# Two half blocks of down-projection weights loaded into unused halves of sum tiles, ahead of the plain step that uses them

## The chip, the cores and the metric

The kernel runs on one core of one Trainium2 chip. The metric is the device time in microseconds (us), median of several executions. Before the change it is 1205.56 us (three runs, 1204.94 to 1208.27).

The core has a matrix engine (PE in the profile, with its weight loads as PEld), a vector engine (DVE), a scalar engine (ACT), a general engine (POOL), and SP, which here does nothing but issue loads and stores. Each engine works through its own queue of instructions in order and waits there for what an instruction needs.

## The reference, cut to what matters

The reference is one layer of a hybrid decoder: a combined input projection, retention and mLSTM heads, an output projection, and a gated feed-forward network with a causal convolution. The change lies in the last product of the feed-forward network.

```python
u = rmsnorm(h, norm_ffn)
up = causal_dwconv(u @ w_up, ffn_conv_w, ffn_conv_b)       # 2048 -> 2 x 5632
gate, val = jnp.split(up, [5632], axis=-1)
return h + (jax.nn.silu(gate) * val) @ w_down              # 5632 -> 2048
```

There are 256 output rows, two tiles of 128. A last norm follows, and 16 meta tokens at the front are dropped.

## The kernel before, in words

**Precision.** All products are made from two parts. A block of weights comes from memory as float32 into a tile `wraw`. ACT copies it to a rounded type (`whi`), DVE subtracts that copy from the block and rounds what is left (`wlo`), and PE multiplies three times: high by high, high by low, low by high. So each block of weights costs one load, one copy on ACT, one subtraction on DVE, and its matmuls. `load_w` (L113 to L122) does that for whole blocks; its copy is L119 and its subtraction L121. `split` (L763) does it for other tiles, with the copy at L764 and the subtraction at L766.

**Stages.** The feed-forward network goes in two halves of the hidden width. Each half has an up-projection (weights `wu`) and then a down-projection (weights `wd`). A down-projection goes through two pairs of column blocks, `b = 0` and `b = 2`, each of 512 columns twice. A pair has eleven steps `q`, each over 256 hidden rows.

**Two kinds of steps.** Four of the steps (0, 4, 9, 10) are plain: for each of the two column blocks, `j = 0` and `j = 1`, a block of 128 x 1024 values (512 KB) is loaded by `load_step` (L909, which calls `load_w`) and PE makes 12 matmuls with it, at L828. The other seven (`FAST`: 1, 2, 3, 5, 6, 7, 8) make a Strassen-like step of seven products instead of eight, in `seven` (L830). Such a step loads four parts of weights into one half of the area `left`: one part of 256 KB that was worked out earlier (`kept`, L838), and three parts of 768 KB together (L839). These loads show as `hT` in the profile, since `left` lies where the tile `hT` was. DVE then makes three differences of the parts, two in a tile `ta` of 128 x 1024 (L842) and one in the first half of a tile `tb` of the same size (L843). The second half of `tb` is used by nobody. Four splits (L764 and L766) and 21 matmuls (L857, L858, L860) follow.

So in the order of steps, runs of seven-product steps alternate with plain steps: 0, then 1 2 3, then 4, then 5 6 7 8, then 9 10. The very last pair of the kernel (second half, `b = 2`) has another order, 0 1 4 2 7 3 5 6 8 9 10, with 7 and 8 plain, and the `j = 1` blocks of its last four plain steps are put off to the end.

**What the tiles share.** `wraw`, `ta` and `tb` are all tiles of one ring of four (`name="wraw", bufs=4`). A new one can be written only when the readers of an older one are through. `whi` and `wlo` are rings of five each. `left` has two halves that alternate, so a seven-product step can load only when the step two before it has read its half.

**What sets the order.** The kernel is written in program order, and a planner orders the instructions of each engine by a simulated timeline and adds the waits. `tc.issue_after(x)` adds that an instruction of a block stands behind `x` on the same engine. The planner also orders SP's loads: in the trace, the load of step 5 can stand ahead of the loads of step 4. While a down-projection runs, POOL adds finished results of the pair before to `hn`, by transfers that accumulate (L876).

Of the kernel before, what the change touches and what calls it, by code (L numbers as in the profile page):

```python
# [11 lines left out]
F32R = mybir.dt.float32r  # L12
# [4 lines left out]
P = 128  # L17
# [66 lines left out]
def trunk(ctx: ExitStack, tc: tile.TileContext, io, out: bass.AP):  # L84
    nc = tc.nc

    def pool(name, bufs, **kw):
        return tc.tile_pool(name=name, bufs=bufs, **kw)

    consts = ctx.enter_context(pool("consts", 1, side="left"))  # L90
    wpool = ctx.enter_context(pool("wpool", 1, side="left"))
# [21 lines left out]
    def load_w(src, shape, to=None):  # L113
        nonlocal last_load
        raw = wpool.tile(shape, F32, name="wraw", bufs=4)
        last_load = nc.sync.dma_start(raw, src)
        to, n = (wpool, 5) if to in (None, wpool) else (to, None)
        hi = to.tile(shape, F32R, name="whi", bufs=n)
        nc.scalar.copy(hi, raw)  # L119
        lo = to.tile(shape, F32R, name="wlo", bufs=n)  # L120
        nc.vector.tensor_tensor(out=lo, in0=raw, in1=hi.bitcast(F32), op=ALU.subtract)  # L121
        return hi, lo  # L122
# [83 lines left out]
    with pool("sq", 1, side="right") as sqp:  # L206
        for k0, k1 in [(0, 1), (1, 2)] + [(k, k + 2) for k in range(2, KT, 2)]:
            n = k1 - k0
# [3 lines left out]
            raw = wpool.tile([P, 2, W0], F32, name="wraw", bufs=4)[:, :n, :]  # L212
# [16 lines left out]
            for k in range(k0, k1):  # L229
                i = k - k0  # L230
                first, last = k == 0, k == KT - 1
                for j, (ps, t0) in enumerate(((k_ps, 0), (q_ps, TQ))):
                    w = hi[:, :, j * P : (j + 1) * P], lo[:, :, j * P : (j + 1) * P]
# [36 lines left out]
    with tc.issue_after(parted.ins):  # L270
        a = _COLS["retn"][0]
        nc.vector.tensor_scalar(out=norms[:, :RH], in0=par[:, a : a + RH], scalar1=-0.5, scalar2=None, op0=ALU.mult)

        a = _COLS["mln"][0]
# [318 lines left out]
    NQD = NHF // 2  # L593
# [74 lines left out]
    def x_tile(i):  # L668
        return x5[:, i, :]
# [23 lines left out]
    def squares(tt, i, c0, c1):  # L693

        nc.scalar.activation(junk[:, : c1 - c0], hn[:, tt, c0:c1], AF.Square, scale=DM ** -0.5, accum_out=ss4[:, tt, i : i + 1])

    def times_gain(tt, c0, c1):
        h = hn[:, tt, c0:c1]
        nc.gpsimd.tensor_tensor(out=h, in0=h, in1=gfin[:, c0:c1], op=ALU.mult)
# [44 lines left out]
    for half in range(2):  # L744
# [18 lines left out]
        def split(hi, lo, x, after=None):  # L763
            copied = nc.scalar.copy(hi, x)  # L764
            with tc.issue_after(after.ins) if after else nullcontext():
                return copied, nc.vector.tensor_tensor(out=lo, in0=x, in1=hi.bitcast(F32), op=ALU.subtract)  # L766

        gt = None
        for jj in range(NHF):
            j = half * NHF + jj  # L770
            pair = []
            for s in range(2):
# [7 lines left out]
                if 2 * jj + s in begins:  # L780
                    n = begins.index(2 * jj + s)
                    b, q = units[n]
# [6 lines left out]
            q, i = divmod(jj, 2)  # L789
# [37 lines left out]
            for n, (a, m, i) in list(enumerate(parts))[n0:n1]:  # L827
                nc.tensor.matmul(ps, a, m[:, i, cols], start=first and n == 0, stop=seed or last and n == 5, skip_group_check=seeded)  # L828

        def seven(b, q, cs, ps, first, last, after, norm):  # L830


            nonlocal turn
            f = FAST.index(q)
            raw = left[turn]
            turn = 1 - turn

            nc.sync.dma_start(raw[:, 0, :], early[b, q])  # L838
            nc.sync.dma_start(raw[:, 1:4, :], io["wd7"][b // 2, half * NQD + q][:, 1:4, :])  # L839
            ta, tb = (wpool.tile([P, 2, 512], F32, name="wraw", bufs=4) for _ in range(2))  # L840

            nc.vector.tensor_tensor(out=ta, in0=raw[:, 0:1, :].to_broadcast([P, 2, 512]), in1=raw[:, 1:3, :], op=ALU.subtract)  # L842
            nc.vector.tensor_tensor(out=tb[:, 0, :], in0=raw[:, 3, :], in1=raw[:, 0, :], op=ALU.subtract)  # L843
            copied = None
            for w, to in (
                (raw[:, 2:4, :], ((S4, cs[0, 1], False, False), (A12, cs[0, 0], False, False))),
                (raw[:, 0:2, :], ((S2, ps[2], first, last), (A11, ps[0], first, last))),
                (ta, ((S3, ps[1], first, last), (S1, ps[3], first, last))),
                (tb[:, 0:1, :], ((A22, cs[1, 0], False, False),)),
            ):  # L850
                hi = wpool.tile([P, 2, 512], F32R, name="whi", bufs=5)
                lo = wpool.tile([P, 2, 512], F32R, name="wlo", bufs=5)
                n = len(to)
                with tc.issue_after(after.ins) if first and after else nullcontext():
                    copied, _ = split(hi[:, :n, :], lo[:, :n, :], w)
                for i, (m, o, begin, _) in enumerate(to):
                    nc.tensor.matmul(o, sh[:, f, m, :], hi[:, i, :], start=begin, stop=False)  # L857
                    nc.tensor.matmul(o, sl[:, f, m, :], hi[:, i, :], start=False, stop=False)  # L858
                for i, (m, o, _, end) in enumerate(to):
                    nc.tensor.matmul(o, sh[:, f, m, :], lo[:, i, :], start=False, stop=end)  # L860
            if norm:

                with tc.issue_after(copied.ins):
                    for g in norm:
                        squares(*g)
                reached = nc.gpsimd.tensor_tensor(out=junk[:, 0:1], in0=tb[:, 0, 0:1], in1=tb[:, 0, 0:1], op=ALU.add)
                with tc.issue_after(reached.ins):
                    for tt, _, c0, c1 in norm:
                        times_gain(tt, c0, c1)
# [4 lines left out]
        def onto(tt, b, x):  # L874

            nc.gpsimd.dma_start(block(tt, b), x, accum_op=ALU.add)  # L876

        def share(ps, b, final):

            p1, p7, p6, p5 = ps  # L880
            x6, x7, x5, x1 = (x_tile(i) for i in range(4))
            nc.scalar.copy(x1, p1)  # L882
            onto(0, b, x1)
            nc.vector.tensor_tensor(out=x6, in0=p6, in1=x1, op=ALU.add)
            nc.vector.tensor_tensor(out=x7, in0=p7, in1=x6, op=ALU.add)
            onto(1, b, x7)
            nc.vector.tensor_tensor(out=x6, in0=x6, in1=p5, op=ALU.subtract)
            if final:

                nc.vector.tensor_tensor(out=block(0, b + 1), in0=block(0, b + 1), in1=x6, op=ALU.add)  # L890
            else:
                onto(0, b + 1, x6)
            nc.vector.tensor_tensor(out=x5, in0=x7, in1=p5, op=ALU.subtract)
            onto(1, b + 1, x5)
# [14 lines left out]
        def load_step(b, q, to=wpool):  # L909
            return load_w(io["wd"][b, half * NQD + q], [P, 2, 512], to)  # L910
# [3 lines left out]
        emptied = None  # L914
        for b in (0, 2):
            cs = {}
            for j in range(2):
                for tt in range(2):
                    cs[tt, j] = at.tile([P, 512], F32, name="atps")
            ps = [mm.tile([P, 512], F32, name="mmps") for _ in range(4)]  # L920

            final = half == 1 and b == 2
            steps = [0, 1, 4, 2, 7, 3, 5, 6, 8, 9, 10] if final else range(NQD)
            fast = [q for q in steps if q in FAST and not (final and q in BOTH)]
            plain = [q for q in steps if q not in fast]
            alone = plain[-lag:] if final else []
            for q in steps:
                if q in fast:
                    due = []
                    if final and q != fast[0]:  # L930
                        due, gains = gains[:1], gains[1:]
                    seven(b, q, cs, ps, q == fast[0], q == fast[-1], emptied, due)
                    if q == fast[-1]:
                        with tc.high_priority() if final else nullcontext():
                            share(ps, b, final)
                    continue
                for j in range(2):
                    if j == 1 and q in alone:
                        continue
                    w = load_step(b + j, q)  # L940
                    for tt in range(2):
                        product(cs[tt, j], tt, q, w, q == plain[0], q == plain[-1 - (lag if final and (tt, j) == (1, 1) else 0)])
            for j in range(2):
                for n, tt in enumerate(range(2)):
                    c = (b + j) * 512
                    if not final:

                        x = x_tile((4, 3, 1, 0)[2 * j + n])
                        emptied = nc.scalar.copy(x, cs[tt, j])
                        onto(tt, b + j, x)  # L950
                        if half == 1:
                            gains.append((tt, b + j, c, c + 512))
                    elif j == 0:
                        add(cs[tt, j], tt, c)
                        squares(tt, b, c, c + 512)
                        times_gain(tt, c, c + 512)
# [116 lines left out]
```

## Time and profile before

| | before |
|---|---|
| median of three runs | 1205.56 us |
| profiled execution, its own time | 1206.01 us |
| its span (first to last instruction) | 1204.2 us |
| PE busy | 1194.5 us, 99% of the span |
| DVE busy | 971.1 us, 81% |
| ACT busy | 708.1 us, 59% |
| granted PE clock | 0.998 |
| down-projection, first half, `b = 0` and `b = 2` | about 717.5 to 773 and 773 to 828.5 us |
| down-projection, second half, `b = 0` and `b = 2` | about 1083 to 1138 and 1138 to 1197 us |

The times inside the profile are microseconds from the start of the span. A row such as `wlo<-wraw,whi` names the tile that is written and the tiles that are read. Matmuls overlap each other, so a matmul's own duration is longer than the distance from its start to the next one's start; the distance is what counts for the pace. What stands in square brackets is the idle time before an instruction and what ended it. An "x2" in a row of the timeline means that two instructions of one kind were merged.

### The profile page before, as it was taken

How to read it: one execution, taken by the hardware profiler on the slowest of the kernel's cores; microseconds unless marked ns; L12 is line 12 of the kernel's file. 1: busy time of each engine (PE TensorE's matmuls, PEld its weight loads, DVE VectorE, ACT ScalarE, POOL GpSimd, SP SyncE). 2: the span in 40 equal slices, each digit the busy share in tenths (PEclk: the TensorE clock that was granted, in tenths of full speed). 3: DMA queues.
4: the chain of work that ended last, by engine and by line, in shares of the span. 5: the costliest groups of instructions: out<-in, count | busy, mean ns of one | idle time of the engine just before them, and what ended most of it. 6: DMA issues, size and time to landing. Idle time of an engine off the chain costs nothing.

```text
span 1204.2 us, 22798 instructions
## 1 busy us (share of the span) xinstructions
PE 1194.5 (99%) x8956; PEld 1151.2 (96%) x8956; DVE 971.1 (81%) x1446; ACT 708.1 (59%) x964; POOL 167.3 (14%) x222
## 2 busy tenths in 40 slices
PE   9999999999999999999999999999999999999997
PEld 9999999999999999999999998878999999998886
DVE  8967778766775966788888889997697878789897
ACT  8747746655656656555555556665554655556664
POOL 0100001111110311021112100202023112100232
PEclk9999999999999999999999999999999999999999
DMA  8865565566565965766866744949777767755956
GB/s 280 275 208 162 169 187 169 197 182 192 171 189 168 345 204 176 252 219 203 263 217 212 225 178 175 272 182 272 279 249 250 234 247 242 253 184 211 281 170 200
DMA packets 83005, 263.27 MB, mean 219 GB/s; under 512 B 14673, under 2 KB 18897, under 8 KB 82769
## 3 DMA queue, kind: packets, MB, share of 16 engines
q1 hardware_dynamic: 71952, 223.85, 56.9%
q0 software_dynamic: 10368, 37.11, 10.1%
q8 instruction: 70, 1.15, 0.4%
q10 hardware_dynamic: 576, 0.85, 0.2%
q14 instruction: 39, 0.31, 0.1%
HBM read 243.42 MB, written 11.27 MB: 211 GB/s over the span
## 4 chain that ended last, share of the span: by engine, by line
PE 97%; DMA 1%; DVE 1%; ACT 0%; issue 0%; SPq 0%; DVEq 0%; ACTq 0%
PE mmps L128 26%; PE mmps L129 25%; PE mmps L131 25%; PE atps L828 8%; PE mmps L860 2%; PE mmps L857 2%; PE mmps L858 2%; PE atps L858 1%; PE atps L857 1%; PE atps L860 1%; PE atps L380 1%; DMA wraw<-in_wd 1%; PE atps L372 0%; DMA hT<-in_xT 0%; PE atps L128 0%; PE atps L131 0%
## 5 line engine op out<-in xcount | busy, mean ns | idle before, releaser
L119 ACT CAST whi<-wraw 128x1024 fp32r<-128x1024 f32 x352 | 368.5, 1049 | 311.0 <-PE mmps L129 200.9
L121 DVE TENSOR_TENSOR wlo<-wraw,whi 128x1024 fp32r<-128x1024 f32 x352 | 432.5, 1231 | 68.9 <-ACT whi L119 66.7
L128 PE MATMUL mmps<-uh,whi 128*128 128x258 f32 x1408 | 346.1, 283 | 0.0
L129 PE MATMUL mmps<-ul,whi 128*128 128x258 f32 x1408 | 346.0, 283 | 0.0
L128 PEld LDWEIGHTS mmps<-uh,whi 128*128 128x128 f32 x1408 | 267.6, 190 | 0.1
L129 PEld LDWEIGHTS mmps<-ul,whi 128*128 128x128 f32 x1408 | 267.1, 190 | 0.1
L128 PE MATMUL mmps<-xh,whi 128*128 128x272 f32 (+2 forms) x864 | 219.8, 288 | 0.0
L129 PE MATMUL mmps<-xl,whi 128*128 128x272 f32 (+2 forms) x864 | 218.3, 286 | 0.0
L131 PE MATMUL mmps<-uh,wlo 128*128 128x258 f32 x1408 | 196.5, 282 | 0.0
L131 PEld LDWEIGHTS mmps<-uh,wlo 128*128 128x128 f32 x1408 | 179.9, 189 | 0.0
L129 PEld LDWEIGHTS mmps<-xl,whi 128*128 128x128 f32 x864 | 162.9, 189 | 0.0
L128 PEld LDWEIGHTS mmps<-xh,whi 128*128 128x128 f32 x864 | 162.5, 188 | 0.1
L131 PE MATMUL mmps<-xh,wlo 128*128 128x272 f32 (+2 forms) x864 | 126.6, 285 | 0.0
L131 PEld LDWEIGHTS mmps<-xh,wlo 128*128 128x128 f32 x864 | 114.2, 188 | 0.0
L764 ACT CAST whi<-hT 128x1024 fp32r<-128x1024 f32 x52 | 53.6, 1052 | 26.5 <-PE atps L828 7.9
L681 DVE TENSOR_TENSOR cu<-mmps,rstd 128x258 f32<-128x258 f32 x88 | 37.3, 424 | 38.1 <-PE mmps L131 37.5
L766 DVE TENSOR_TENSOR wlo<-hT,whi 128x1024 fp32r<-128x1024 f32 x52 | 62.2, 1221 | 5.9 <-ACT whi L764 4.7
L129 PE MATMUL mmps<-mixl,whi 128*128 128x258 f32 x256 | 63.0, 283 | 0.0
L128 PE MATMUL mmps<-mixh,whi 128*128 128x258 f32 x256 | 62.4, 282 | 0.0
L766 DVE TENSOR_TENSOR wlo<-wraw,whi 128x1024 fp32r<-128x1024 f32 (+1 forms) x52 | 52.2, 1038 | 0.9 <-PE mmps L860 0.2
L764 ACT CAST whi<-wraw 128x1024 fp32r<-128x1024 f32 (+1 forms) x52 | 43.0, 837 | 16.5 <-PE mmps L858 7.1
L876 POOL DMA_DIRECT2D hn<-x x27 | 23.6, 1033 | 202.6 <-ACT x L882 174.8
(284 smaller groups left out, 1732.9 us busy)
## 6 DMA issues: line engine op xcount, KB each, us to landing
wraw<-in_wu SPq DMA_DIRECT2D x176, 512.0 KB, 4.5
wraw<-in_wi SPq DMA_DIRECT2D x108, 512.0 KB, 4.1
hT<-in_wd SPq DMA_DIRECT2D x26, 768.0 KB, 4.6
wraw<-in_wd SPq DMA_DIRECT2D x36, 512.0 KB, 4.9
wraw<-in_wo SPq DMA_DIRECT2D x32, 512.0 KB, 4.1
x<-in_wd POOLq DMA_DIRECT2D x13, 768.0 KB, 7.5
hn<-x POOLq DMA_DIRECT2D x27, 256.0 KB, 7.9
hT<-kept SPq DMA_DIRECT2D x26, 256.0 KB, 2.8
```

Of the source, the lines that this page charges most:

```text
L119: nc.scalar.copy(hi, raw)
L121: nc.vector.tensor_tensor(out=lo, in0=raw, in1=hi.bitcast(F32), op=ALU.subtract)
L128: nc.tensor.matmul(ps, hi[:, k, :], xh(kk), start=kk == first, stop=False)
L129: nc.tensor.matmul(ps, hi[:, k, :], xl(kk), start=False, stop=False)
L131: nc.tensor.matmul(ps, lo[:, k, :], xh(kk), start=False, stop=kk == last)
L681: evacuated = nc.vector.tensor_tensor(out=u, in0=ps[:, :NQ], in1=rstd2, op=ALU.mult)
L764: copied = nc.scalar.copy(hi, x)
L766: return copied, nc.vector.tensor_tensor(out=lo, in0=x, in1=hi.bitcast(F32), op=ALU.subtract)
L828: nc.tensor.matmul(ps, a, m[:, i, cols], start=first and n == 0, stop=seed or last and n == 5, skip_group_check=seeded)
L857: nc.tensor.matmul(o, sh[:, f, m, :], hi[:, i, :], start=begin, stop=False)
L858: nc.tensor.matmul(o, sl[:, f, m, :], hi[:, i, :], start=False, stop=False)
L860: nc.tensor.matmul(o, sh[:, f, m, :], lo[:, i, :], start=False, stop=end)
```

## The change

The plain step behind a run of at least two seven-product steps no longer loads its `j = 0` block into a `wraw` tile of its own. The block's two halves, 128 x 512 values each (256 KB), go into the unused second halves of the `tb` tiles of the last two steps of that run. Both are asked for in the last step of the run, behind that step's own load on SP. The block is then split in two instructions of 512 columns on ACT and two on DVE in place of one each of 1024. The `j = 1` block is loaded as before.

The condition holds at seven places: step 4 and step 9 in both pairs of the first half and in the first pair of the second half, and step 8 in the last pair. So seven loads of 512 KB become fourteen of 256 KB.

```diff
-        def seven(b, q, cs, ps, first, last, after, norm):
+        def seven(b, q, cs, ps, first, last, after, norm, pieces):
...
             nc.sync.dma_start(raw[:, 0, :], early[b, q])
-            nc.sync.dma_start(raw[:, 1:4, :], io["wd7"][b // 2, half * NQD + q][:, 1:4, :])
+            asked = nc.sync.dma_start(raw[:, 1:4, :], io["wd7"][b // 2, half * NQD + q][:, 1:4, :])
             ta, tb = (wpool.tile([P, 2, 512], F32, name="wraw", bufs=4) for _ in range(2))
+            for n, i in pieces:
+                if i == 0:
+                    spare.append(tb[:, 1, :])
+                else:
+                    spare.append(tb[:, 1, :])
+                    for i, x in enumerate(spare):
+                        with tc.issue_after(asked.ins):
+                            nc.sync.dma_start(x, io["wd"][b, half * NQD + n][:, i, :])
...
-            for q in steps:
+            spare = []
+            for n, q in enumerate(steps):
                 if q in fast:
...
-                    seven(b, q, cs, ps, q == fast[0], q == fast[-1], emptied, due)
+                    pieces = [(steps[n + 2 - i], i) for i in range(2)
+                              if steps[n + 2 - i] in plain and all(m in fast for m in steps[n - i : n + 2 - i])]
+                    seven(b, q, cs, ps, q == fast[0], q == fast[-1], emptied, due, pieces)
...
-                    w = load_step(b + j, q)
+                    if j == 0 and spare:
+                        w = [wpool.tile([P, 2, 512], F32R, name=name, bufs=5) for name in ("whi", "wlo")]
+                        for i, x in enumerate(spare):
+                            split(*(a[:, i, :] for a in w), x)
+                        spare = []
+                    else:
+                        w = load_step(b + j, q)
```

## The prediction

> **What bounds the kernel now.** I read the page first, then PE's waits, then the chain of waits, and last the timelines of PE, ACT, DVE and SP around the places that these name.
>
> ```profile
> span 1204.2 us, 22798 instructions
> PE 1194.5 (99%) x8956; PEld 1151.2 (96%) x8956; DVE 971.1 (81%) x1446; ACT 708.1 (59%) x964; POOL 167.3 (14%) x222
> ...
> PE atps L199 <- DVE ones L169: 1.1, 1, 1.1
> PE atps L828 <- ACT whi L119: 0.8, 2, 0.4
> PE atps L128 <- ACT whi L226: 0.3, 1, 0.3
> ```
>
> PE works through 99% of the span. Its whole list of waits has three rows, and two of these are at the kernel's start. The one that the change can reach is the middle one: matmuls of a plain step (L828) that wait for ACT's copy of a loaded block (L119), twice. These are both places:
>
> ```profile
> 791.94 0.62 PE L860 MATMUL mmps<-wlo,sh 128*128 128x512 f32 x2
> 792.93 0.51 PE L828 MATMUL atps<-whi,mh 128*128 128x512 f32 x1 [0.36 <-ACT whi L119]
> ...
> 793.51 0.40 PE L828 MATMUL atps<-whi,mh 128*128 128x512 f32 x1
> 793.74 0.40 PE L828 MATMUL atps<-whi,ml 128*128 128x512 f32 x1
> ...
> 817.32 0.63 PE L860 MATMUL mmps<-wlo,sh 128*128 128x512 f32 x2
> 818.36 0.50 PE L828 MATMUL atps<-whi,mh 128*128 128x512 f32 x1 [0.42 <-ACT whi L119]
> ...
> 818.94 0.39 PE L828 MATMUL atps<-whi,mh 128*128 128x512 f32 x1
> ```
>
> Undisturbed, one matmul starts 0.23 us after the other (793.51 to 793.74). From 791.94 to 793.51 four are started, which is 0.92 us of work in 1.57: 0.65 us lost. From 817.32 to 818.94 again four, 0.92 in 1.62: 0.70 us lost. They are steps 4 and 9 of the second pair of the first half, two of the seven places that the change touches. A third has a smaller loss without a wait row, step 8 in the last pair:
>
> ```profile
> 1176.03 0.50 PE L828 MATMUL atps<-whi,sh 128*128 128x512 f32 x1
> 1176.36 0.40 PE L828 MATMUL atps<-whi,sl 128*128 128x512 f32 x1
> 1176.60 0.39 PE L828 MATMUL atps<-whi,sh 128*128 128x512 f32 x1
> ```
>
> Two matmuls in 0.57 in place of 0.46: 0.11 us. At the other four places PE has no wait, so nothing can be won there.
>
> What is behind the two waits stands in the chain and on ACT:
>
> ```profile
> 786.95 1.15 DVE wlo L766
> 788.11 3.62 DMA wraw<-in_wd
> ...
> 791.83 1.05 ACT L119 CAST whi<-wraw 128x1024 fp32r<-128x1024 f32 x1 [3.03 <-DMA wraw<-in_wd]
> 817.26 1.05 ACT L119 CAST whi<-wraw 128x1024 fp32r<-128x1024 f32 x1 [2.82 <-DMA wraw<-in_wd]
> ```
>
> The load of step 4 waits until DVE has read an older tile of the ring (788.11), takes 3.62 us, and the copy 1.05. This is the trap of the chain: it books 3.62 us to the load, but PE had other matmuls in most of that time. What the load costs is PE's loss, 0.65 us.
>
> **The change part by part.**
>
> *The load goes earlier.* The pieces need no ring slot of their own, only that the second half of `tb` is free, and SP must have passed the step's own load.
>
> ```profile
> 778.09 1.03 SPq L839 DMA_DIRECT2D hT<-in_wd  x1
> 782.48 0.33 SPq L838 DMA_DIRECT2D hT<-kept  x1
> ...
> 777.60 1.82 DVE L766 TENSOR_TENSOR wlo<-wraw,whi 128x1024 fp32r<-128x1024 f32 x2
> ```
>
> Step 3's own load is asked for at 778.09. Its `tb` goes into the slot that step 1's `tb` leaves when DVE has read it, at 777.60 + 1.82 = 779.42. So the pieces are issued at about 779.4, 8.7 us before the 788.11 of today. SP then waits until 782.48 for its next load anyway, so a wait of the pieces on SP up to there holds up nobody.
>
> *Their landing.* They queue behind step 3's load, which has a landing of its own that matters:
>
> ```profile
> hT<-in_wd SPq DMA_DIRECT2D x1, 768.0 KB, 6.9
> ...
> 785.12 1.23 DVE L842 TENSOR_TENSOR wraw<-hT 128x1024 f32<-128x1024 f32 x1 [2.67 <-DMA hT<-in_wd]
> ...
> 788.51 0.62 PE L860 MATMUL mmps<-wlo,sh 128*128 128x512 f32 x2
> ```
>
> The first row is of the window 777 to 779: the load lands 6.9 us after 778.09, at 785.0, and DVE, which has it next in its queue, stands still for 2.67 us. A later landing would push all that follows on DVE. How much do two loads close behind slow one down? In the windows around 726.94 (two loads of 512 KB issued 1.0 and 1.6 us behind it) and 717.59 (nothing behind it) the same load shows:
>
> ```profile
> hT<-in_wd SPq DMA_DIRECT2D x1, 768.0 KB, 4.7
> ...
> hT<-in_wd SPq DMA_DIRECT2D x1, 768.0 KB, 4.4
> ```
>
> That is 0.3 us for twice the bytes. The other bound is even sharing: 512 KB at the pace of the 768 KB in 4.4 us would be 2.9 us later, if all of it went first. The first low part that DVE makes after its wait is ready at 786.95 + 1.15 = 788.10 (the chain's row), and PE uses it at 788.51, so 0.41 us are free there. I take 0: the near row is 0.3 and lies under the cover. The far bound would cost 2.9 − 0.4 = 2.5 us, at this place; where DVE does not stand and wait for the step's load, it costs nothing.
>
> [...]
>
> *The split.* Two instructions in place of one, on two engines:
>
> ```profile
> L119 ACT CAST whi<-wraw 128x1024 fp32r<-128x1024 f32 x24 | 25.2, 1050 | 25.5 <-DMA wraw<-in_wd 18.3 <-DMA wraw<-in_wu 7.2
> L764 ACT CAST whi<-wraw 128x512 fp32r<-128x512 f32 x14 | 8.7, 621 | 4.9 <-PE atps L828 2.0 <-PE mmps L858 1.5 <-DVE wlo L766 1.1
> L121 DVE TENSOR_TENSOR wlo<-wraw,whi 128x1024 fp32r<-128x1024 f32 x25 | 30.3, 1221 | 7.2 <-ACT whi L119 7.0 <-PE mmps L860 0.2
> L766 DVE TENSOR_TENSOR wlo<-wraw,whi 128x512 fp32r<-128x512 f32 x14 | 9.6, 686 | 0.1
> ...
> 773.00:828.50 55.50, 54.72 (x238) 44.29 (x237) 50.23 (x52) 34.20 (x40) 7.00 (x8) 1.00 0.68 206
> ```
>
> ACT: 2 x 0.621 − 1.050 = 0.19 us more at each place. ACT is busy 34.20 of 55.5 us in this stage, so that is hidden. DVE: 2 x 0.686 − 1.221 = 0.15 us more, and DVE is busy 50.23 of 55.5, close behind PE. The tightest place that I find:
>
> ```profile
> 814.24 2.36 DVE L766 TENSOR_TENSOR wlo<-hT,whi 128x1024 fp32r<-128x1024 f32 x2
> ```
>
> DVE ends this pair of low parts at 816.60, and PE uses the second from 817.32: 0.72 us of cover. With step 4's wait gone PE is there 0.65 earlier, and DVE 0.15 later: 0.08 short. So 0.08 us is given back.
>
> *What is late next.* Behind the copies, the low part of the plain block:
>
> ```profile
> 792.61 1.22 DVE L842 TENSOR_TENSOR wraw<-hT 128x1024 f32<-128x1024 f32 x1
> 793.75 1.22 DVE L121 TENSOR_TENSOR wlo<-wraw,whi 128x1024 fp32r<-128x1024 f32 x1
> 818.34 1.22 DVE L121 TENSOR_TENSOR wlo<-wraw,whi 128x1024 fp32r<-128x1024 f32 x1
> ...
> 797.41 1.08 PE L828 MATMUL atps<-wlo,mh 128*128 128x512 f32 x4
> 822.84 1.54 PE L828 MATMUL atps<-wlo,mh 128*128 128x512 f32 x6
> ```
>
> DVE has it (L121) at 794.97 and 819.56, PE uses it 2.4 and 3.3 us later; of that 0.65 and 1.35 go, with the first place's gain carried on. So it holds. The `j = 1` block now takes the slot that the `j = 0` block took, so its load is issued at 788.11 and no longer behind another. What is held longer is the slot of each `tb`: until the plain block is split, where it was until the step's last split. The next users are the differences of step 5 or the second load of step 10. Step 5's first difference stands on DVE ahead of the plain block's subtraction today, at 792.61; if it must stand behind, it comes 1.2 us later (a subtraction of the row above), and its own use lies behind the 5.5 us of the plain step's 24 matmuls (24 x 0.23). I cost that at nothing.
>
> **The sum.** 0.65 + 0.70 + 0.11 − 0.08 = 1.38 us won, from 1206.01 of the profiled execution (span 1204.2 and 1.8 around it), gives 1204.6. The median shown is 0.45 under the profiled execution, so the forecast is 1205.56 − 1.38 = 1204.2 us. Less than 0.3% (3.6 us) of difference is about what a measurement of this kernel cannot tell from none, so this is "the same".
>
> **The rivals.**
>
> *Nothing arrives early, or the gain is eaten.* The order on SP is the planner's, and "behind the step's load" is only a lower bound: the pieces may stand behind the next step's load too, or DVE, busy for 91% of the stage, may set the pace anyway. For it: the 50.23 of 55.5 us. Against it: the 8.7 us of lead, and the cover of 0.72. If the far bound of the landing holds it is −1.38 + 2.5 = +1.1. So 1205.0 to 1206.7, about 1205.6.
>
> *Slower: a piece's split stands ahead of the last step's own splits on DVE or ACT.* The planner puts it there if its timeline has the pieces landed earlier than they land, and then both queues wait for a landing as DVE does at 785.12, for 2.67 us. It begins to cost from 0.72 us on. Price per place: 2.67 − 0.72 = 1.95. At three of the seven, 5.9 − 1.4 = +4.5: 1210.0 us. For it: the order is made from estimated times, and a load of 4.4 us took 6.9 here. Against it: the pieces are asked for 8.7 us earlier than the load that they replace, and the ring of five `whi` tiles holds the split back until PE is through with the tile five before, so it can't stand far ahead.
>
> *Faster: the chain's reading.* Removing load and copy from the chain would be worth 3.62 + 1.05 us at the first place, and as much at the second: 9.3 us, 1196.2. Against it: PE's waits hold 0.8 us, not 9.
>
> **How the numbers follow.** Forecast 0.63, gain eaten 0.25, slower 0.10 (0.09 of it over 0.3%), chain's reading 0.02. So faster 0.02, the same 0.89, slower 0.09. The forecast's own range is 1203.2 to 1205.4, by the spread of the runs before and the terms of the sum. The range that should hold 8 in 10 takes in the eaten gain and half a slower case: 1202.9 to 1207.2.
>
> **What would show it.** In the changed profile PE's waits have no row for L828 behind a copy at the seven places; SP shows two issues of 256 KB into `wraw` behind each last load of a run, about 779.4 at the first stall; DVE's idle time before the step's difference (2.67) stays what it is; the copies of 128x512 for plain steps no longer end a PE wait. The prediction is wrong if PE's busy share falls, if a new wait on a low part (`wlo`) shows in PE's list at steps 3, 5 or 8, or if the first stall is there with the pieces landed.

## The result and the profile after

The changed kernel takes 1213.24 us (median of six runs, 1211.74 to 1214.91), the kernel before 1207.66 us in the runs beside it (six, 1204.94 to 1208.91). The ratio is 1.005, with a 95% interval of 1.0037 to 1.0063. So the change makes the kernel slower by about 0.5%, 5.6 us; the forecast was 1204.2 us, no measurable difference.

The profiled execution took 1211.74 us, with a span of 1210.0 (before: 1206.01 and 1204.2), at a granted clock of 0.998 in both. The head of the page after, and PE's whole list of waits (us in total, times, longest):

```profile
span 1210.0 us, 22837 instructions
PE 1196.6 (99%) x8956; PEld 1151.3 (95%) x8956; DVE 971.5 (80%) x1453; ACT 708.4 (59%) x971; POOL 167.9 (14%) x222
...
PE atps L828 <- ACT whi L119: 2.1, 2, 1.2
PE atps L828 <- DVE wlo L121: 1.2, 2, 0.7
PE atps L828 <- ACT x L966: 1.2, 1, 1.2
PE atps L199 <- DVE ones L169: 1.1, 1, 1.1
```

The work is the same but for the split blocks (seven more instructions on ACT and on DVE), and PE's waits inside the stages have gone from 0.8 to 4.5 us. Every new row is at L828, the plain steps. L966 is the copy that empties PE's sums at the end of a pair (L949 before). A wait on PE cost somewhat more than its idle time here (0.93 us at 768.82 cost 1.19 in all), so I also count, for each matmul from 600 us on, by how much it starts later than the pace of its kind behind the one before it. Before, that is 1.55 us in all; after, 7.22. The difference, 5.67 us, is the 5.8 us of the spans. It lies here:

```
where (us)        what PE waits for                          lost, us
768.8             copy of step 10's j = 0 block, 1st pair    1.19
775.8             sums not emptied, start of 2nd pair        1.47
829.7             copy of step 10's j = 1 block, 2nd pair    1.46
1193.5, 1195.9    low parts of the put-off j = 1 blocks      1.77
elsewhere                                                    1.33
```

None of these is one of the seven places of the change. The two stalls that the change aimed at are gone: PE's timeline after, at step 4 of the second pair, and at step 9 of it, has no idle time before the plain step's first matmuls. (Of the 0.70 us at step 9, 0.25 comes back 1.5 us later, at 821.15, where PE waits for the copy of its `j = 1` block, done at 821.09.)

```profile
794.91 0.39 PE L828 MATMUL atps<-whi,mh 128*128 128x512 f32 x1
...
819.64 0.39 PE L828 MATMUL atps<-whi,mh 128*128 128x512 f32 x1
```

Where the first new stall comes from can be followed backwards. DVE's timeline behind step 4 in the first pair of the first half (start, duration), first before, then after:

```profile
733.31 1.22 DVE L842 TENSOR_TENSOR wraw<-hT 128x1024 f32<-128x1024 f32 x1
734.45 0.68 DVE L843 TENSOR_TENSOR wraw<-hT 128x512 f32<-128x512 f32 x1
735.05 2.35 DVE L121 TENSOR_TENSOR wlo<-wraw,whi 128x1024 fp32r<-128x1024 f32 x2
737.33 1.22 DVE L766 TENSOR_TENSOR wlo<-hT,whi 128x1024 fp32r<-128x1024 f32 x1
738.46 1.22 DVE L842 TENSOR_TENSOR wraw<-hT 128x1024 f32<-128x1024 f32 x1
739.60 1.22 DVE L766 TENSOR_TENSOR wlo<-hT,whi 128x1024 fp32r<-128x1024 f32 x1
```

```profile
733.36 1.22 DVE L850 TENSOR_TENSOR wraw<-hT 128x1024 f32<-128x1024 f32 x1
734.49 1.29 DVE L766 TENSOR_TENSOR wlo<-wraw,whi 128x512 fp32r<-128x512 f32 x2
735.70 1.22 DVE L121 TENSOR_TENSOR wlo<-wraw,whi 128x1024 fp32r<-128x1024 f32 x1
736.83 0.69 DVE L851 TENSOR_TENSOR wraw<-hT 128x512 f32<-128x512 f32 x1
738.32 1.22 DVE L850 TENSOR_TENSOR wraw<-hT 128x1024 f32<-128x1024 f32 x1 [0.80 <-DMA hT<-in_wd]
739.46 1.22 DVE L766 TENSOR_TENSOR wlo<-hT,whi 128x1024 fp32r<-128x1024 f32 x1
...
741.20 1.22 DVE L766 TENSOR_TENSOR wlo<-hT,whi 128x1024 fp32r<-128x1024 f32 x1
```

The planner has made another order. Before, step 6's first difference (L842 at 738.46) stood between step 5's two subtractions (L766 at 737.33 and 739.60). After, step 6's difference (L850) stands ahead of both, and waits 0.80 us for step 6's load, which lands at 738.20 (before: 737.85, when DVE had not come to it yet). Step 5's second subtraction ends at 742.42 in place of 740.82, and with it step 5's half of `left` comes free, into which step 7 loads. SP's timelines show the loads that follow, first before, then after:

```profile
740.84 0.33 SPq L838 DMA_DIRECT2D hT<-kept  x1
741.22 0.42 SPq L839 DMA_DIRECT2D hT<-in_wd  x1
...
759.85 4.02 SPq L116 DMA_DIRECT2D wraw<-in_wd  x4
```

```profile
742.45 0.33 SPq L838 DMA_DIRECT2D hT<-kept  x1
742.87 0.80 SPq L839 DMA_DIRECT2D hT<-in_wd  x1
...
761.52 3.27 SPq L116 DMA_DIRECT2D wraw<-in_wd  x4
```

Step 7's load goes out 1.6 us later, and the four last plain loads (step 10's two, and step 0's two of the next pair) begin 1.67 us later; the loads of the next pair's steps 1 and 2 between them are late by as much (755.02 and 760.76 in place of 753.41 and 759.09). At this end of the pair there is little room. ACT's copies of the first and the last of these four blocks, its emptying of the sums, and PE's matmuls that need them, before and then after:

```profile
762.15 0.58 ACT L882 COPY x<-mmps 128x512 f32<-128x512 f32 x1
765.61 1.05 ACT L119 CAST whi<-wraw 128x1024 fp32r<-128x1024 f32 x1 [2.88 <-DMA wraw<-in_wd]
...
771.24 1.06 ACT L119 CAST whi<-wraw 128x1024 fp32r<-128x1024 f32 x1 [1.60 <-DMA wraw<-in_wd]
772.20 2.14 ACT L949 COPY x<-atps 128x512 f32<-128x512 f32 x4
...
767.68 0.39 PE L828 MATMUL atps<-whi,mh 128*128 128x512 f32 x1
773.17 0.39 PE L828 MATMUL atps<-whi,mh 128*128 128x512 f32 x1
```

```profile
767.72 1.04 ACT L119 CAST whi<-wraw 128x1024 fp32r<-128x1024 f32 x1 [4.47 <-DMA wraw<-in_wd]
...
774.20 1.05 ACT L119 CAST whi<-wraw 128x1024 fp32r<-128x1024 f32 x1 [1.50 <-PE atps L828]
775.15 2.04 ACT L966 COPY x<-atps 128x512 f32<-128x512 f32 x4
...
768.82 0.50 PE L828 MATMUL atps<-whi,mh 128*128 128x512 f32 x1 [0.93 <-ACT whi L119]
775.78 0.50 PE L828 MATMUL atps<-whi,mh 128*128 128x512 f32 x1 [1.20 <-ACT x L966]
```

Before, the first copy is done at 766.66 and PE uses it at 767.68: 1.02 us of cover. After, it is done at 768.76, 2.10 us later: 1.08 too late, and with the slower second matmul that is the 1.19 us lost. The emptying of the sums stands behind the fourth copy on ACT. Before, its first copy ends at 772.20 + 0.58 = 772.78 and PE needs it at 773.17, a cover of 0.39 us. After, the fourth load, asked for at 764.46 in place of 763.54, takes 9.6 us in place of 7.6, and the copy and the emptying wait for it: 1.47 us lost. (The row of that copy names PE, whose last signal came at 774.14. But the load lands at 774.10, 0.10 us before the copy begins, as at 771.14 and 771.24 before, and the `whi` tile that it writes was last used by step 9's first block, which PE had long left. Before and after, POOL's accumulations onto `hn`, issued from 763.04 and 763.55 on, are under way while the last of these loads land.) The second pair repeats it: its step 10 loads go out 3.46 and 4.06 us later than before, of which 2.6 are the lateness that PE brings along, and step 10's second load takes 6.1 us in place of 4.3.

### The profile page after: what moved, and what is told of

Read it like the earlier page. It is cut to its first block, busy times and chain, and to the rows that moved or that the text cites. A ratio compares the mean times of both kernels' runs of the same rounds, so it can differ in the third digit from the quotient of the medians.

```text
span 1210.0 us, 22837 instructions
## 1 busy us (share of the span) xinstructions
PE 1196.6 (99%) x8956; PEld 1151.3 (95%) x8956; DVE 971.5 (80%) x1453; ACT 708.4 (59%) x971; POOL 167.9 (14%) x222
## 5 line engine op out<-in xcount | busy, mean ns | idle before, releaser
L119 ACT CAST whi<-wraw 128x1024 fp32r<-128x1024 f32 x345 | 360.8, 1048 | 298.4 <-PE mmps L129 185.3
L121 DVE TENSOR_TENSOR wlo<-wraw,whi 128x1024 fp32r<-128x1024 f32 x345 | 424.3, 1231 | 70.6 <-ACT whi L119 69.0
L766 DVE TENSOR_TENSOR wlo<-hT,whi 128x1024 fp32r<-128x1024 f32 x52 | 62.0, 1218 | 4.2 <-ACT whi L764 2.9
L764 ACT CAST whi<-wraw 128x1024 fp32r<-128x1024 f32 (+1 forms) x66 | 50.6, 790 | 19.7 <-PE mmps L866 5.6
L766 DVE TENSOR_TENSOR wlo<-wraw,whi 128x1024 fp32r<-128x1024 f32 (+1 forms) x66 | 60.9, 961 | 0.4 <-ACT whi L764 0.2
L828 PE MATMUL atps<-whi,mh 128*128 128x512 f32 (+1 forms) x132 | 51.1, 389 | 3.3 <-ACT whi L119 2.1
```

## The experiments

The theory behind the first runs was this: the new order on DVE behind step 4 makes step 7's load late, and by it the loads of steps 10 and 0; the put-off loads at the end have a cause of their own, the slot of the ring that a piece holds. The rivals were that the split itself, the pieces' traffic, or the places one by one are to blame. In each diff the plus lines are the experiment's. "Lost" is PE's count as above. Every kernel here is planned anew as a whole, so a diff of a line also moves instructions elsewhere.

**One kind of place at a time.** The change only at step 4 (three places), only at step 9 (three), only at step 8 of the last pair (one).

```diff
-                              if steps[n + 2 - i] in plain and all(m in fast for m in steps[n - i : n + 2 - i])]
+                              if steps[n + 2 - i] == 4 and steps[n + 2 - i] in plain and all(m in fast for m in steps[n - i : n + 2 - i])]
```

> Pieces only for step 4 (three places); steps 9 and 8 load as before. Theory A (the planner's new order on DVE behind step 4, with step 6's difference ahead of step 5's subtractions, makes step 7's load and all behind it late, down to step 10): PE stalls of about 1 us at step 10 of the first pair and about 1 us at the start of the second pair stay, step 7's load goes out about 1.6 us later than before, and the kernel is 2 to 4 us slower than before. Theory B (the slots of the tb tiles held at step 9 make the loads of step 10 and of the next pair late): no stall at step 10, 0.6 us faster than before.

Measured: 1208.79 us against 1206.72, ratio 1.0024 (1.0012 to 1.0036). Step 7's load goes out at 742.42, late as with the whole change (742.87). But in its profile, of an execution that took 1212.83 us, PE's largest loss is not at step 10. It is 3.0 us at 764.55, at step 9: that step's loads go out at 757.11 in place of 755.84, and the first takes 6.2 us in place of 3.8. So lateness costs here too, at another place.

> Pieces only for step 9 (three places). Theory A: step 7's load goes out when it did before, no stall at step 10 of the first pair, the stall in front of step 9 of the second pair (0.70 us) is gone: 0.5 to 0.8 us faster than before, same within the noise. Theory B: the second load of step 10 and the two loads of the next pair's step 0 wait for the held slots, PE stalls 1 to 1.5 us at each of step 10 and step 0: 2 to 4 us slower.

Measured (with `== 9`): 1206.48 against 1206.72, ratio 1.0002 (0.9993 to 1.0011). The stall of step 9 is gone, that of step 4 is there (0.81 us lost at 793.33), and step 7's load goes out at 741.44, near the 741.22 of before. The 0.5 to 0.8 us that were expected to be won do not show in the median.

> Pieces only for step 8 of the last pair (one place). If the 2.6 us that PE loses in the last 10 us of the changed kernel come from the held slots there: about 2 us slower than before, with PE waits for the low parts of the last plain blocks. If they come from what happened earlier (other contention, other order): no difference to before, 0.1 us either way.

Measured (with `== 8`): 1209.24 against 1206.72, ratio 1.0018 (1.0009 to 1.0027). The first row of PE's waits in this run:

```profile
PE atps L828 <- DVE wlo L121: 1.2, 2, 0.7
```

It is the wait at the end, on the low parts of the put-off blocks. What follows: 0.24%, 0.02% and 0.18% add up to the whole 0.50% within their intervals. Step 9's places cost nothing measurable by themselves, and so, at those places, does all that they share with the others: the split in two, the pieces' transfers, the longer-held `tb`. Step 4's places and step 8's cost something each.

**The order on DVE, set by hand.** The whole change, and step 6's first difference is held behind step 5's second subtraction. This is not the order of before, where the difference stood between the two subtractions, but a third one, in which both stand ahead of it.

```diff
-            nc.vector.tensor_tensor(out=ta, in0=raw[:, 0:1, :].to_broadcast([P, 2, 512]), in1=raw[:, 1:3, :], op=ALU.subtract)
+            with tc.issue_after(behind.ins) if q == 6 and (half, b) != (1, 2) else nullcontext():
+                nc.vector.tensor_tensor(out=ta, in0=raw[:, 0:1, :].to_broadcast([P, 2, 512]), in1=raw[:, 1:3, :], op=ALU.subtract)
...
-                    copied, _ = split(hi[:, :n, :], lo[:, :n, :], w)
+                    copied, parted = split(hi[:, :n, :], lo[:, :n, :], w)
+                if to[0][0] == S2:
+                    behind = parted
```

> The whole change, and step 6's first difference on DVE put behind step 5's second subtraction by hand (all pairs but the last). Theory A: step 7's load goes out 2 to 3 us earlier than in the changed kernel, the stalls at step 10 and at the next pair's start shrink to under 0.5 us each, and the kernel is 2 to 3 us faster than the changed one, 2 to 3 us slower than before with the rest at its end. Theory B: step 7's load is earlier, but the stalls at step 10 and at the start of the next pair stay at over 1 us; time as the changed kernel's.

Measured: 1208.97 against 1206.72, ratio 1.002 (1.001 to 1.003), where the change alone has 1.005. Lost: 2.55 us in place of 7.22. DVE behind step 4:

```profile
736.87 0.69 DVE L852 TENSOR_TENSOR wraw<-hT 128x512 f32<-128x512 f32 x1
737.48 2.36 DVE L766 TENSOR_TENSOR wlo<-hT,whi 128x1024 fp32r<-128x1024 f32 x2
739.75 1.22 DVE L851 TENSOR_TENSOR wraw<-hT 128x1024 f32<-128x1024 f32 x1
```

Step 5's subtractions (L766) now end at 739.84 and step 7's load goes out at 740.28, 0.9 us earlier than before the change. The stalls of the first pair are gone but for 0.1 us. What is left is 0.79 us at step 10 of the second pair, where under 0.5 was expected, and 1.5 us at the end.

**The slot at the end.** Only step 8's place, but its pieces go into a tile of their own, so no slot of the ring is held.

```diff
-                    spare.append(tb[:, 1, :])
+                    own = more.tile([P, 2, 512], F32, name="own", bufs=1) if half == 1 else None
+                    spare.append(tb[:, 1, :] if own is None else own[:, 0, :])
...
-                    spare.append(tb[:, 1, :])
+                    spare.append(tb[:, 1, :] if own is None else own[:, 1, :])
```

> As the kernel with the pieces of step 8 alone, but they land in a tile of their own and no slot of the ring is held for them. If the held slots cost the 2 us at the end (theory: the first put-off load behind step 10 then waits for a piece's split), the loss goes: 0 to 0.4 us faster than before, no PE wait on the low parts of the last plain blocks. If the splitting in halves or the early loads cost it, it stays 2 us slower.

Measured: 1206.46 against 1207.0, ratio 1.0006 (0.9993 to 1.0019). The wait on the put-off low parts (L121) is no longer in PE's list, which runs from the first of these rows to the second, with the kernel's start left out:

```profile
PE atps L828 <- ACT whi L119: 1.1, 2, 0.6
...
PE mmps L869 <- DVE wlo L766: 0.2, 1, 0.2
```

With the held slot (the run of step 8 alone) the first put-off load goes out at 1177.32, as soon as DVE has read a piece (1177.25), and takes 5.8 us where the kernel before has 1176.83 and 4.1. The three behind it are asked for when they were before (1177.92 to 1182.03) and land 1.3 us later. So the wait at the end is the held slot's, shown by its going with the slot. That the slot is all of the 0.18% is likely, but the two intervals overlap.

**Both remedies.** The order set by hand and step 8 left out; then the order set by hand, all seven places, and a tile of their own for the pieces of the second half.

> The changed kernel without its place in the last pair, and with step 6's first difference put behind step 5's second subtraction. Theory A (order on DVE is what cost in the first three pairs, the place in the last pair is a second cost by itself): the sum of both losses is gone, within 1 us of before on either side. If the places at steps 4 and 9 cost something besides that order: 1.5 us or more slower than before.

Measured: 1207.98 against 1207.0, ratio 1.0011 (1.0001 to 1.002). Lost: 4.64 us in its profile, 1.61 of them at 1142.1 and 0.84 at 774.0, both on the emptying of the sums.

> All seven places, step 6's first difference put behind step 5's second subtraction, and in the second half the pieces land in a tile of their own. If order and held slots are the two costs, both are gone and the won stalls are left: 0.5 to 1.4 us faster than before. If a third cost stands behind them: slower than that, 1 us or more.

Measured: 1207.1 against 1207.0, ratio 1.0 (0.9991 to 1.0009). Lost: 0.64 us, less than the 1.55 of before. The profiled execution has the shortest span of the study (1203.9), but the median shows no gain. So with both remedies the 0.5% is gone. Of the 0.5 to 1.4 us that were expected to be won the median shows nothing: the interval ends at a gain of 0.09%, just short of the predicted 1.38 us (0.11%).

**Is it the order, or the held slots behind the order?** All seven places, the own tile in the second half, and the planner's own order.

> All seven places, the planner's own order, and in the second half the pieces in a tile of their own, so that no slot of the ring is held there. If the held slots make the planner put step 6's difference first: the second half has the order of before and loses nothing (PE's lost time after 1080 us under 0.3 us). If not: step 6's difference still stands first there, DVE waits for step 6's load at about 1104 us, and PE loses 1 us or more at about 1135 to 1145 us, while the loss in the last 15 us is gone. In both cases the first half loses its 3 to 4 us as in the changed kernel, and the whole is 2.5 to 5 us slower than before.

Measured: 1209.3 against 1207.24, ratio 1.0017 (1.0006 to 1.0029). In the second half, where no slot of the ring is held, DVE still has step 6's difference ahead of step 5's subtractions (it waits there at 1104.33). So the held slot isn't what turned the planner's order round. What did is left open. PE lost nothing after 1080 us in this profile, though, where 1 us or more was expected with this order. And in the first pair DVE meets step 6's load already landed, step 7's load goes out at 741.80 and step 10's first at 759.36, and PE loses nothing there either. So the order need not cost. The profiled execution took 1206.42 us here, 2.9 under the median, so its rows say little of the median. But the median itself is 2.1 us slower than before where 2.5 to 5 were expected: the tile of their own took 0.33% off the whole 0.50%, the order set by hand 0.30%, and both together no more than the 0.50%. So the costs of slots and order don't seem to be simply added.

**The order alone, in the kernel before.** Both ways. First the bad order without any piece: step 6's load and differences are written ahead, and step 5's two subtractions held behind them.

```diff
-                    copied, _ = split(hi[:, :n, :], lo[:, :n, :], w)
+                    copied, _ = split(hi[:, :n, :], lo[:, :n, :], w, heads[6][3].get(to[0][0]) if q == 5 and 6 in heads else None)
...
```

> The kernel before, without any piece, with only DVE's order behind step 4 made that of the changed kernel: step 6's first difference ahead of step 5's first subtraction, its second ahead of step 5's second. Theory A: DVE waits there for step 6's load, step 7's load goes out 1.0 to 1.6 us later than before (before: 741.2), step 10's loads about as much, and PE stalls 0.5 to 1.2 us at step 10 of the first pair: 1 to 3 us slower than before. If the order is harmless without the pieces: no difference, under 0.5 us.

Measured: 1210.35 against 1207.0, ratio 1.0021 (1.0012 to 1.003). Step 7's load goes out at 743.86 (before: 741.22). So the order costs about as much as step 4's places, without the pieces. But the stalls don't all lie where they lie in the changed kernel: 0.62 us at step 9, 1.24 on the emptying of the sums at 1141.6, none at step 10 of the first pair. Then the other way, the kernel before with the difference held behind both subtractions, as in the run with the order set by hand.

> The kernel before, without any piece, with step 6's first difference put behind step 5's second subtraction. It tells whether the hand-set order is worth something by itself, which would have to be taken off what it won in the changed kernel. If it only undoes the changed kernel's order: no difference to before, the two stalls of 0.65 and 0.70 us in the second pair stay, within 0.5 us. If it helps by itself (step 7's load goes out 1 to 2 us earlier than before, and the loads of step 9 with it): 0.5 to 1.5 us faster.

Measured: 1211.82 against 1207.24, ratio 1.0039 (1.0026 to 1.0052). Since this is not the order of before, it undoes nothing. It is a third order, and a costly one, and that I can't square with "late loads cost, early ones don't". Step 7's load goes out at 740.33, 0.9 us earlier than before, the orders on SP, ACT and POOL are those of before, DVE's differs in nine instructions and PE's in some two dozen, and yet it is slower than anything but the change itself. Its PE waits:

```profile
PE atps L828 <- ACT x L952: 4.5, 2, 2.3
...
PE atps L828 <- ACT whi L119: 1.0, 1, 1.0
```

L952 is the emptying of the sums (L949). This run also limits what the one with both remedies shows. That one has the same order and is level with before; the order without the change is 0.39% slower than before. So the two remedies took the loss away, but it isn't shown that the two causes are the whole of it.

In its profile the loads of the crowded stretch go out earlier and land later: the last of them is asked for at 763.02 and lands at 775.55, where the kernel before has 763.54 and 771.14. To see what of this is the kernel and what the single execution, both were profiled once more.

> The kernel before, with step 6's first difference held behind step 5's second subtraction, profiled a second time. In its first profile the loads of step 8 and of step 10 that were asked for at 758.3 to 763.0 took 5 to 12.5 us to land where the kernel before has 3.0 to 7.6, and PE stood still for 1.00 us at 769.1, 2.35 us at 777.2 and 2.19 us at 1145.9. If these waits come from this kernel's own order of DVE, its loads land as late again at the same places: the step 8 load in over 6 us and a wait of PE behind an evacuation copy (L952) of over 1.5 us at one of the two places, time 1211 to 1214 us. If they are chance of that one execution, the loads land in 3 to 7.6 us, the wait is under 0.5 us at both, and time is 1206 to 1208.5 us.

Measured: 1208.66 us against 1207.17, one run each. The same waits are there, smaller at the first place: 0.73 us at 773.9 in place of 2.35, and 1.96 at 1141.6 in place of 2.19. So the late landings seem to belong in part to this kernel, and the time lies between the two that were expected. (The load at 758.3 that the expectation calls step 8's is that of step 2 of the next pair.)

```profile
PE atps L828 <- ACT x L952: 2.7, 2, 2.0
...
PE atps L828 <- ACT whi L119: 0.4, 1, 0.4
```

> The kernel before, unchanged, profiled a second time, for the spread of one load from execution to execution. If the cover of 0.33 us at step 10 decides, its load (759.85 in the first profile) lands 5.3 to 6.0 us later and PE loses under 0.5 us there; PE loses about 1.5 us in all from 600 us on, at steps 4 and 9 of the second pair of the first half, and the time is 1205 to 1208 us. If landings are as loose as in the kernel with the order alone, a stall of over 0.5 us shows at another place than these two.

Measured: 1206.51 us, span 1204.7, lost 1.55 us. The 0.33 us of this expectation is a misreading of mine: the matmul that I took for the first use of step 10's block belongs to the block before, and the cover is the 1.02 us shown above. Step 10's load takes 5.3 us here (5.7 in the first profile), and PE does not wait there. The fourth load takes 8.4 us (asked for at 763.83, landed at 772.24) in place of 7.6, and the emptying behind its copy is ready too late for PE, which loses 0.30 us at 773.92:

```profile
772.34 1.05 ACT L119 CAST whi<-wraw 128x1024 fp32r<-128x1024 f32 x1 [2.48 <-DMA wraw<-in_wd]
773.29 2.04 ACT L949 COPY x<-atps 128x512 f32<-128x512 f32 x4
```

So the 0.39 us of cover at the start of the next pair is used up by chance alone in one execution of the kernel before out of two. In both profiles of the difference held back without the change the fourth load lands later although it is asked for earlier (12.5 and 9.6 us). Early asking is not the reason by itself: with both remedies at all seven places it is asked for 0.65 us earlier than before and lands 0.53 us earlier. The transfers show the place but not the reason. Windows of two microseconds, the last two columns the DMA engines' busy share and GB/s, first before, then the difference held back, then that kernel a second time:

```profile
758.00:760.00 2.00, 2.00 (x11) 1.63 (x10) 2.00 (x3) 0.30 (x1) 0.00 (x0) 1.00 1.00 400
760.00:762.00 2.00, 2.00 (x11) 1.63 (x10) 1.64 (x2) 1.55 (x2) 0.00 (x0) 1.00 1.04 370
```

```profile
758.00:760.00 2.00, 2.00 (x11) 1.63 (x10) 1.98 (x3) 1.06 (x1) 0.00 (x0) 1.00 0.81 245
760.00:762.00 2.00, 2.00 (x11) 1.63 (x10) 1.37 (x2) 1.10 (x2) 0.00 (x0) 1.00 0.55 171
```

```profile
758.00:760.00 2.00, 2.00 (x11) 1.63 (x10) 1.51 (x2) 1.24 (x2) 0.00 (x0) 1.00 0.92 271
760.00:762.00 2.00, 2.00 (x11) 1.63 (x10) 1.83 (x2) 1.38 (x2) 0.00 (x0) 1.00 0.99 337
```

Loads are waiting in all of these windows, POOL's accumulations have not begun, and the engines move 171 to 337 GB/s in place of 370 to 400. Why they move less is open.

## Why the prediction was wrong

**What bounds the kernel: right.** PE's own waits in the stages held 0.8 us, which cost 1.55 us by the count above, and no more than that was to be had there. The two stalls are gone with the change, and the loss of 3.62 + 1.05 us per place that the chain of waits suggests was never there. (At the second place, moreover, the chain's own rows hold 3.41 + 1.06 us and not as much as at the first.) With both remedies the kernel is at 1.000 of before, 0.9991 at best. That rules out the 0.8% of the chain's reading, and leaves the predicted 0.11% unseen.

**The load goes earlier, and its landing: right but for small sizes.** The pieces of step 4 in the second pair go out 1.1 and 2.2 us behind step 3's load. I had 1.3. They land at 788.87 and 789.51, before PE comes to them. SP has passed the second at 783.54, and its next load follows at 785.20. Step 3's load lands after 7.3 us in place of 6.9; I had put 0.3 us to this from the near bound and taken 0 because of the cover. DVE waits 3.17 in place of 2.67 us for it, and PE loses 0.23 us behind that, at 791.36; the far bound of 2.9 us is out at this place. So the landing is 0.4 us later than before, and one pair of executions can't tell whether these are the pieces' or the spread of landings.

**The split: right.** Two subtractions of a piece take 1.29 us together (734.49), where one of the block takes 1.22: 0.07 us more, where I had 0.15. The 0.08 us that I gave back for it ahead of step 9 does not show there; the 0.25 us at 821.15 was not in the sum. Step 9's places alone cost nothing measurable.

**"What is late next" is the step that failed.** I asked what stood behind the plain block's low part, named the right suspects (the longer-held `tb` slot, "the differences of step 5 or the second load of step 10"), and wrote "I cost that at nothing" after looking at one of them in one place. Two things went wrong in it.

First, I argued from the order on DVE as it was, with one instruction moved by 1.2 us. The planner made a new order behind step 4, with step 6's difference in front of step 5's subtractions and a wait for step 6's load in it. That is 1.6 us on step 7's load and 2.10 on step 10's first copy, against a cover of 1.02 that I never read, and beyond it the emptying of the sums, with 0.39. Holding the difference behind both subtractions took the whole from 1.005 to 1.002 and the lost time from 7.22 to 2.55 us; making the planner's new order without pieces cost 0.21%. That both happen is shown. That lateness of the loads alone is the whole mechanism is not: the kernel before is slower by 0.39% also when its loads behind step 6 go out earlier, and with tiles of their own the second half had the new order and lost nothing in its profile.

Second, the slot. I looked for its next user in the first half. In the last pair the piece's slot is waited for by the put-off loads, and PE waits for their low parts, 1.77 us. A tile of its own removes that wait, and the 0.18% of step 8's place is no longer seen (1.0006, 0.9993 to 1.0019).

**The rivals.** The slower one came out near the size (1210.0 against 1213.2), but not by its mechanism: no piece's split waits for a landing in the profile after, and the instruction in front is a difference, not a split. Its evidence, that the planner's order is made from estimated times and a load can take 6.9 us in place of 4.4, was the right thing to look at; I bounded it with the ring of five `whi` tiles, which says where splits can stand and nothing of the differences. "Eaten" named the planner's order too, but on SP.

**What would show it.** Of the signs named, a wait on a low part is in PE's list (1.2 us), at the put-off blocks at the end of the kernel. At the seven places no copy of a `j = 0` block holds PE up any more, but DVE's wait before the step's difference did not stay at 2.67 us. The largest losses lie at steps 10 and 0, which I had not listed at all.

## What to carry to other kernels

Where a planner orders the engines from estimated times, a moved load is not one moved load: list, for every engine, the waits that hold with less than a microsecond of cover up to the end of the stage, and price the change against the thinnest of them, not against the place that it edits. Undisturbed rows are no proof of room: read the cover as the use less the end of what feeds it, before the change, at the ends of stages above all, where loads, copies and emptied sums meet. And a change worth 0.1% by its own sum is best tried place by place, since one harmful place hides the harmless ones. An order that is set by hand to undo a side effect is a change of its own: run it without the change too.

## What the runs showed of the hardware

**The landing time of one load spread from 7.6 to 12.5 us at one place.** The 512 KB load of step 0's `j = 1` block, issued between 762.6 and 764.5, took 7.6 and 8.4 us in two executions of the kernel before, 9.6 in the changed kernel, 7.7 with both remedies at all seven places, and 12.5 and 9.6 us with the difference held back in the kernel before. The same form took 4.3 us at 818.36 in the kernel before, 2.2 us ahead of POOL's first accumulation there (820.52).

**Two stalls of PE cost more than themselves.** After the 2.35 us of idle time at 777.23 in the first profile with the difference held back in the kernel before, PE ran at full pace for 1.4 us and then at half. Its windows behind that stall:

```profile
777.00:778.80 1.80, 1.57 (x7) 1.25 (x8) 1.80 (x2) 1.80 (x5) 1.33 (x3) 0.96 0.00 0
778.80:782.20 3.40, 3.40 (x10) 2.68 (x9) 3.40 (x5) 3.19 (x4) 2.19 (x3) 0.52 1.05 184
782.20:785.60 3.40, 3.40 (x17) 2.79 (x16) 1.85 (x3) 1.09 (x2) 0.00 (x0) 1.00 1.07 195
```

The column before the last two is the granted clock: 0.52 for 3.40 us, with ten matmuls, where the next 3.40 us have seventeen at 1.00. From 778.79 to 782.15 eight are started, 1.84 us of work at the pace of 0.23, in 3.36: about 1.5 us lost on top of the 2.5. The stall of 2.19 us at 1145.9 is followed by the same 3.4 us, at 0.51. (The other four of that kernel's first five executions have a mean granted clock of 0.997 to 0.999, 0.996 here, and still take 1211.39 to 1213.36 us; so the clock hardly explains its loss of 0.39%.) The stall of 2.75 us at 764.6 in the run with step 4 alone was not followed by it (the clock is 1.00 up to 774.0), and neither was the 1.96 us in the repeat (1.00 up to 1150.0). So the length of the stall doesn't decide.

The traces show more. The stretch of full clock that is recorded takes 1194.67 us in the trace of before and 1198.08 us after: 3.41 us apart, and 350 and 351 times 3.413 us. The two stretches of half clock begin at 778.67 and 1147.31, 368.64 us apart, which is 108 times that. In the 3.41 us right ahead of each of the two (775.26 to 778.67, and 1143.90 to 1147.31) PE was idle for 1.97 and 1.98 us. What sets these two stalls apart from the longer one of 2.75 us, behind which the clock stayed at 1.00, is not shown.
